# A hybrid decoder layer: state products, state update and masked products of each scan chunk issued in one run, and a reordered first layer norm

## The chip, the cores and the metric

The kernel runs on one core of a Trainium2 chip. The core has a matrix engine (TensorE, PE in the profile, with its weight loads as PEld), a vector engine (VectorE, DVE), a scalar engine (ScalarE, ACT), GpSimd (POOL) and SyncE (SP), which only issues DMAs here. Each engine works through its own instructions in order; between engines they wait by semaphores. The metric is the time of one execution on the device in microseconds, the median of several executions. Lower is better.

## What is computed

One layer: a layer norm at the input, a wide input projection, a conformer branch (a 31-tap causal convolution along time), a Mamba-2 state space branch in chunks of 128 positions, their gated mix with an output projection and a layer norm, and a gated feed-forward part with a short convolution. There are 1024 positions of 1024 channels, 32 heads of 64 channels, 4 groups with a state of 128.

```python
def ssd_chunked(x, dt, a_head, bm, cm):
    ...
    cb = jnp.einsum("bclgn,bcsgn->bcgls", cc, bc)
    y_diag = jnp.einsum("bcgrls,bcsgrp->bclgrp", cb[:, :, :, None] * decay, xs)
    decay_states = jnp.exp(a_cs[..., -1:] - a_cs)
    states = jnp.einsum("bclgn,bcgrl,bclgrp->bcgrpn", bc, decay_states, xs)
    chunk_decay = jnp.exp(a_cs[..., -1])
    ...
    y_off = jnp.einsum("bclgn,bcgrpn,bcgrl->bclgrp", cc, prev, jnp.exp(a_cs))
    return (y_diag + y_off).reshape(b, t, h, p)

def ssd_branch(z, xbc, dt_raw, conv_w, conv_b, dt_bias, a_log, d_skip, norm_w, w_out):
    ...
    xbc = jax.nn.silu(causal_dwconv(xbc, conv_w, conv_b))
    ...
    y = y + xh * d_skip.astype(jnp.float32)[:, None]
    yg = (y.reshape(bsz, t, SSM_DIM) * jax.nn.silu(z.astype(jnp.float32)))
    yg = yg.reshape(bsz, t, SSM_GROUPS, SSM_DIM // SSM_GROUPS)
    yg = yg * lax.rsqrt(jnp.mean(jnp.square(yg), axis=-1, keepdims=True) + RMS_EPS)
    yn = (yg.reshape(bsz, t, SSM_DIM) * norm_w.astype(jnp.float32)).astype(z.dtype)
    return yn @ w_out

def reference(x, ...):
    h = layer_norm(x, ln_in_g, ln_in_b)
    for l in range(DEPTH):
        u = h @ w_in[l]
        u_glu, z, xbc, dt_raw, gate_a, gate_b = split_in(u)
        y_a = conformer_branch(u_glu, ...)
        y_b = ssd_branch(z, xbc, dt_raw, ...)
        mix = (jax.nn.sigmoid(gate_a) * y_a + jax.nn.sigmoid(gate_b) * y_b) @ w_o[l]
        h = layer_norm(DN_ALPHA * h + mix, ln1_g[l], ln1_b[l])
        ffn = conv_ffn(h, w_ffn_up[l], ffn_dw_w[l], ffn_dw_b[l], w_ffn_down[l])
        h = layer_norm(DN_ALPHA * h + ffn, ln2_g[l], ln2_b[l])
    return h
```

## The kernel before

All matrices are f32. A large product is made of three fp32r matmuls of high and low parts (`mm3`, L180 to L182): high by high, high by low, low by high. `project` makes 24 of them, of 512 columns each, for 128 output channels. The high part is a cast on ACT (L146 for weights, L196 for activations), the low part a subtraction on DVE (L147, L197). The 1024 positions are taken in two halves (hh = 0 and 1) of 512.

`ln_first` norms the first half in four tiles of 128 positions, transposes each on TensorE (`hi`, `lo`) and makes the first three columns of the input projection (dt, and B and C of group 0) as soon as tiles are there (`columns`, q = 0 for the first two tiles, q = 1 for the others). On ACT, DVE and TensorE its order is that of the code (`manual_schedule`). Two tiles take their statistics on DVE (`stats`), two on ACT (`sums`).

`mixers` then goes over the four groups. For each group: the columns of B, C and four x tiles, each convolved by `conv4` (ACT and DVE) and passed through SiLU; the pending norm of the group before (`done`, which is `normed`); two columns of the conformer's gated unit; the scan of the group (`ssd_group`); the group's z gate (`z_gate`); and two pieces of the 31-tap convolution (`conv31`, L536 on DVE, 30 rows per piece), which have a low priority and fill DVE. For group 3 the first half of the scan's output projection (`ssm_out_first`, weights so_0 to so_7) stands ahead of it. `combine` makes the gate columns gb and the second half of that projection (sp_0 to sp_7), then the conformer's norm (mean at L763, variance) and its output.

A chunk of `ssd_group` is: four transposes of x (L584), a transpose of B (L587), CB (L590); on ACT the decay mask `m` (L598, L602) and the weighted x `xsd` (L613); on DVE the causal CB (`cbm`, L604), `xs` (L606) and the masked product `m` times `cbm` (L614); on TensorE four products with the carried state (`po`, L619), the state update (`pn`, L623) and eight masked products (`py`, L633), and on DVE the sums behind them (L620, L627, L630, L643). After four chunks come the skip (L648), the gate product with the SiLU of z (L652), squares and their sum (L654 to L658). `normed` sums them by channels on TensorE (L663), takes the root (L668, L669), sends the result through DRAM (`r_scr`, L671 and L672) so that it lies in all partitions, scales the tiles (L675) and splits them into `yT`.

The order of the instructions outside `manual_schedule` is set by the tile scheduler from priorities and an estimated timeline; the small products of a chunk are therefore strewn among the projections, which do not depend on them. Buffers bound how far the engines may part: four PSUM banks "acc" for projections, four "sm" for small products, three weight tiles, five `zs`, twelve `xbc`, two `m`, one `ys`.

Of the kernel before, what the change touches and what calls it, by code (L numbers as in the profile page):

```python
# [8 lines left out]
F32 = mybir.dt.float32  # L9
F32R = mybir.dt.float32r  # L10
AF = mybir.ActivationFunctionType
ALU = mybir.AluOpType
# [4 lines left out]
P = 128  # L17
D = 1024
# [26 lines left out]
RW_ING, RW_INB, RW_1G, RW_1B, RW_2G, RW_2B = (i * D for i in range(6))  # L45
# [4 lines left out]
CT_A, CT_G, CT_X, CT_B, CT_C, CT_DT, CT_GA, CT_GB = 0, 8, 16, 32, 36, 40, 41, 49  # L50
# [4 lines left out]
def kernel(  # L55
# [15 lines left out]
    V, A, G, TE, SY = nc.vector, nc.scalar, nc.gpsimd, nc.tensor, nc.sync  # L71
# [80 lines left out]
    def raw_weights(ct, name):  # L152
        st = wst.tile([P, D], F32, tag="st", name=f"st_{name}")
        SY.dma_start(st, wcol[ct])
        return st

    def split_weights(st, name):
        w = wsp.tile([P, 2, D], F32R, tag="w", name=f"w_{name}")
        A.copy(w[:, 0, :], st)
        V.tensor_tensor(  # L160
            out=w[:, 1, :], in0=st, in1=w[:, 0, :].bitcast(F32), op=ALU.subtract
        )
        return w
# [54 lines left out]
    def row(pl, start, n, name, tag=None):  # L218
        r = pl.tile([P, n], F32, tag=tag or name, name=name)
        SY.dma_start(r, prow[start : start + n].partition_broadcast(P))  # L220
        return r
# [21 lines left out]
    def ln_apply(t, mv, rs, i, g, b, op=ALU.subtract):  # L243
        V.scalar_tensor_tensor(  # L244
            out=t, in0=t, scalar=mv[:, i, 0:1], in1=g, op0=op, op1=ALU.mult
        )
        V.scalar_tensor_tensor(  # L247
            out=t, in0=t, scalar=rs[:, i : i + 1], in1=b, op0=ALU.mult, op1=ALU.add
        )

    def ln_first():
# [3 lines left out]
        with pool("lnin0", side="right") as pl:  # L255
            xts, raw = [], []
            with tc.high_priority(offset=8000), tc.manual_schedule(
                engines={et.Activation, et.DVE, et.PE}
            ):
                gb = [pl.tile([P, D], F32, name=n) for n in ("in_g", "in_b")]  # L260
                for r, start in zip(gb, (RW_ING, RW_INB)):
                    A.dma_start(r, prow[start : start + D].partition_broadcast(P))
                A.activation(out=pl.tile([P, 1], F32, name="warm"), in_=eps, func=AF.Sqrt)
                for t in range(4):
                    xt = pl.tile([P, D], F32, tag="x", bufs=4, name=f"x0_{t}")
                    SY.dma_start(xt, x[t * P : (t + 1) * P, :])
                    xts.append(xt)
                    if t:
                        raw.append(raw_weights((CT_DT, CT_B, CT_C)[t - 1], f"first{t}"))
                SY.dma_start(pc[:, :PC_N], pcol[:, :PC_N])  # L270
                SY.dma_start(a_log, prow[RW_AL : RW_AL + HEADS].partition_broadcast(P))
                SY.dma_start(nskip.rearrange("p i k -> p (i k)"), pcol[:, PC_N:])
# [12 lines left out]
                def sums(t):  # L285
                    mean, var = mvs[t][:, 0, 0:1], mvs[t][:, 0, 1:2]
                    A.activation(out=work, in_=xts[t], func=AF.Identity, accum_out=var)
                    A.mul(mean, var, -1.0 / D)
                    A.activation(out=work, in_=xts[t], func=AF.Square, bias=mean, accum_out=var)
                    A.activation(out=rss[t], in_=var, func=AF.Sqrt, bias=eps, scale=1.0 / D)  # L290

                def norm(t):
                    V.reciprocal(out=rss[t], in_=rss[t])
                    op = ALU.subtract if t < 2 else ALU.add
                    ln_apply(xts[t], mvs[t], rss[t], 0, *gb, op=op)
                    SY.dma_start(h_scr[0][t * P : (t + 1) * P, :], xts[t])

                def hi(t):
# [31 lines left out]

                stats(0)
                stats(1)
                norm(0)
                hi(0)
                norm(1)
                lo(0)
                ws.append(weights_side_by_side(raw[0], "c0_dt"))
                hi(1)
                lo(1)
                columns(0, 0, ((0, 0), (0, 1)))  # L340
                ws.append(split_weights(raw[1], "c0_b"))
                sums(2)
                columns(1, 0, ((0, 0), (0, 1), (1, 0)))
                norm(2)
                ws.append(split_weights(raw[2], "c0_c"))
                sums(3)
                norm(3)
                hi(2)
                columns(2, 0, ((0, 0), (0, 1), (1, 0)))
# [210 lines left out]
    def ssd_group(pl, hh, g, xT, BT, CT, gate):  # L560
# [16 lines left out]
        for c in range(4):  # L577
# [31 lines left out]
            if not last:  # L609
                xsd = pl.tile([P, HALF], F32, tag="xsd", name=f"xsd{nm}")  # L610
                for h in range(8):
                    hs, k = slice(h * HP, (h + 1) * HP), 8 * g + h
                    A.mul(xsd[:, hs], px[:, hs], dts[1][:, c, k : k + 1])  # L613
            V.tensor_tensor(out=m, in0=m, in1=cbm.unsqueeze(1).to_broadcast([P, 8, P]), op=ALU.mult)  # L614
            if not first:
                po = bank(0)
                for i in range(4):
                    ts = slice(i * P, (i + 1) * P)
                    TE.matmul(po[:, ts], S[:, ts], CT[:, cs], start=True, stop=True)  # L619
                V.tensor_tensor(out=acc[:, :, cs], in0=by_tile(po), in1=acc[:, :, cs], op=ALU.mult)  # L620
            if not last:
                pn = bank(0)
# [9 lines left out]
            for h in range(8):  # L632
                TE.matmul(  # L633
                    py[h % 2 * HP : (h % 2 + 1) * HP, h // 2 * P : (h // 2 + 1) * P],
                    xs[:, h * HP : (h + 1) * HP],
                    m[:, h, :],
                    start=True,
                    stop=True,
                )
            if first:  # L640
                A.copy(acc[:, :, cs], by_tile(py))
            else:
                V.tensor_tensor(out=acc[:, :, cs], in0=acc[:, :, cs], in1=by_tile(py), op=ALU.add)  # L643
# [764 lines left out]
```

## Time and profile before

| | us |
|---|---|
| median of 3 runs | 1956.8 (1955.83 to 1957.99) |
| the profiled execution, own time | 1956.2 |
| its span, first to last instruction | 1954.5 |
| TensorE busy | 1925.0 |
| VectorE busy | 1635.8 |
| ScalarE busy | 1106.4 |
| GpSimd busy | 133.1 |

A row of a timeline has the start, the duration, the engine, the line, the operation, the tiles written and read, the number of equal instructions taken together, and in brackets how long the engine was idle before and what released it. Durations of matmuls overlap, since they are pipelined; the distance of two starts is what one costs. A view of waits has a line for each pair of waiting and released line: the time in total, how often, and the longest.

### The profile page before, as it was taken

The numbers are of one execution on the slowest core, as the hardware profiler recorded it, in microseconds if no ns is written. First come the engines' busy times: TensorE is split into PE (matmuls) and PEld (weight loads), VectorE is DVE, ScalarE is ACT, GpSimd is POOL, SyncE is SP. The second block draws the span as 40 slices with busy tenths as digits, with TensorE's granted clock in tenths as the row PEclk, the third lists the DMA queues.
The fourth block names the chain that finished last, engine by engine and source line by source line (L and its number), as shares of the span: only waits on it lengthen the run. The fifth ranks groups of instructions, "written<-read, shape, count | busy, mean of one in ns | idle before, by whom it ended". The sixth has DMA issues, their size and how long they took to land.

```text
span 1954.5 us, 24929 instructions
## 1 busy us (share of the span) xinstructions
PE 1925.0 (98%) x9128; PEld 1574.9 (81%) x9128; DVE 1635.8 (84%) x2215; ACT 1106.4 (57%) x1841; POOL 133.1 (7%) x184
## 2 busy tenths in 40 slices
PE   6999999999999999999999999999999999999998
PEld 5888888887788887888888888888888888888886
DVE  7699999998666879999999966588998887887778
ACT  5767777565453268867755545365655454453442
POOL 0100000000400010000000040001000000021000
PEclk9999999999999999999999999999999999999999
DMA  6434343534445643434353454477443232377572
GB/s 215 129 114 130 107 137 101 186 115 140 162 135 192 230 122 107 145 109 135 98 177 109 136 180 130 154 265 256 151 162 108 103 113 87 108 242 260 183 252 108
DMA packets 104011, 297.68 MB, mean 152 GB/s; under 512 B 12432, under 2 KB 12464, under 8 KB 103888
## 3 DMA queue, kind: packets, MB, share of 16 engines
q1 hardware_dynamic: 87552, 243.63, 37.2%
q0 software_dynamic: 13744, 47.21, 7.8%
q10 hardware_dynamic: 2592, 5.24, 0.7%
q8 instruction: 71, 1.16, 0.2%
q14 instruction: 52, 0.43, 0.1%
HBM read 246.22 MB, written 49.82 MB: 151 GB/s over the span
## 4 chain that ended last, share of the span: by engine, by line
PE 80%; issue 11%; DVE 4%; ACT 2%; DMA 2%; POOL 1%; SPq 0%; ACTq 0%; DVEq 0%; POOLq 0%
PE acc L181 21%; PE acc L180 21%; PE acc L182 21%; PE sm L180 4%; PE sm L181 4%; PE sm L182 4%; PE sm L633 2%; PE sm L619 1%; PE sm L623 1%; PE sm L584 1%; DMA m<-cum_scr 1%; PE acc L323 1%; DVE rows L244 1%; POOL var L772 0%; DVE rows L247 0%
## 5 line engine op out<-in xcount | busy, mean ns | idle before, releaser
L536 DVE SCALAR_TENSOR_TENSOR c<-v,pc,c 128x512 f32<-128x512 f32 x480 | 344.3, 743 | 6.5 <-ACT c L525 5.3
L180 PE MATMUL acc<-hT,w_c 128*128 128x512 f32 x368 | 147.2, 400 | 0.0
L181 PE MATMUL acc<-hT,w_c 128*128 128x512 f32 x368 | 146.9, 399 | 0.0
L182 PE MATMUL acc<-hT,w_c 128*128 128x512 f32 x368 | 145.0, 394 | 0.0
L598 ACT ACTIVATE m<-m,cums 128x128 f32<-128x128 f32 x256 | 79.0, 396 | 66.1 <-DMA m<-cum_scr 61.8
L1043 DVE SCALAR_TENSOR_TENSOR fo<-u,pc,fo 128x1024 f32<-128x1024 f32 x88 | 111.1, 1285 | 0.0
L491 DVE SCALAR_TENSOR_TENSOR xbc<-u,pc,xbc 128x512 f32<-128x512 f32 x144 | 104.9, 744 | 1.1 <-ACT xbc L489 0.9
L180 PE MATMUL acc<-h1s,w_s 128*128 128x512 f32 x264 | 103.1, 391 | 0.0
L182 PE MATMUL acc<-h1s,w_s 128*128 128x512 f32 x264 | 103.0, 390 | 0.0
L182 PE MATMUL acc<-hT,w_z 128*128 128x512 f32 x256 | 102.8, 402 | 0.0
L181 PE MATMUL acc<-h1s,w_s 128*128 128x512 f32 x264 | 102.7, 389 | 0.0
L180 PE MATMUL acc<-hT,w_z 128*128 128x512 f32 x256 | 101.9, 398 | 0.4 <-ACT sig L512 0.4
L181 PE MATMUL acc<-hT,w_z 128*128 128x512 f32 x256 | 101.2, 395 | 0.0
L1183 ACT CAST w_dn<-dr 128x1024 fp32r<-128x1024 f32 (+1 forms) x73 | 60.8, 842 | 69.5 <-DVE dr L1113 38.5
L181 PEld LDWEIGHTS acc<-hT,w_c 128*128 128x128 f32 x368 | 69.2, 188 | 16.4 <-issue 3.1
L182 PEld LDWEIGHTS acc<-hT,w_c 128*128 128x128 f32 x368 | 69.1, 188 | 15.6 <-issue 1.9
L180 PEld LDWEIGHTS acc<-hT,w_c 128*128 128x128 f32 x368 | 69.2, 188 | 15.5 <-issue 1.9
L1184 DVE TENSOR_TENSOR w_dn<-dr,w_dn 128x1024 fp32r<-128x1024 f32 (+1 forms) x73 | 70.0, 968 | 11.6 <-ACT w_dn L1183 11.4
L147 DVE TENSOR_TENSOR w_c<-st_c,w_c 128x1024 fp32r<-128x1024 f32 x46 | 55.9, 1216 | 19.9 <-ACT w_c L146 19.9
L146 ACT CAST w_c<-st_c 128x1024 fp32r<-128x1024 f32 x46 | 48.3, 1051 | 40.3 <-PE acc L182 17.2
L180 PE MATMUL sm<-h1b,w_s 128*128 128x512 f32 x176 | 69.1, 393 | 0.0
L181 PE MATMUL sm<-h1b,w_s 128*128 128x512 f32 x176 | 69.0, 392 | 0.0
(380 smaller groups left out, 5592.0 us busy)
## 6 DMA issues: line engine op xcount, KB each, us to landing
st_c<-wcol SPq DMA_DIRECT2D x46, 512.0 KB, 3.5
st_z<-wz SPq DMA_DIRECT2D x32, 512.0 KB, 3.6
m<-cum_scr POOLq DMA_DIRECT2D x32, 512.0 KB, 4.9
st_wo<-wo SPq DMA_DIRECT2D x24, 512.0 KB, 4.3
ra<-wup SPq DMA_DIRECT2D x22, 512.0 KB, 3.5
rb<-wup SPq DMA_DIRECT2D x22, 512.0 KB, 3.3
t_scr<-fo POOLq DMA_DIRECT2D x22, 512.0 KB, 3.4
dr<-t_scr SPq DMA_DIRECT2D x44, 256.0 KB, 3.7
```

Source lines behind the costliest of these rows:

```text
L146: A.copy(w[:, 0, :], st)
L147: (eng or V).tensor_tensor(out=w[:, 1, :], in0=st, in1=w[:, 0, :].bitcast(F32), op=ALU.subtract)
L180: TE.matmul(ps, wa(0), xa(0), start=start, stop=False, skip_group_check=more)
L181: TE.matmul(ps, wa(0), xa(1), start=False, stop=False, skip_group_check=more)
L182: TE.matmul(ps, wa(1), xa(0), start=False, stop=stop, skip_group_check=more)
L491: V.scalar_tensor_tensor(out=o, in0=u[:, k : k + HALF], scalar=pc[:, wc + k : wc + k + 1], in1=o, op0=ALU.mult, op1=ALU.add,)
L536: V.scalar_tensor_tensor(out=accs[i], in0=v[:, k : k + HALF], scalar=pc[:, wc + k : wc + k + 1], in1=accs[i], op0=ALU.mult, op1=ALU.add,)
L598: A.activation(out=m[:, h, :], in_=m[:, h, :], func=AF.Relu, scale=-1.0, bias=cums[:, c, k : k + 1],)
L633: TE.matmul(py[h % 2 * HP : (h % 2 + 1) * HP, h // 2 * P : (h // 2 + 1) * P], xs[:, h * HP : (h + 1) * HP], m[:, h, :], start=True, stop=True,
L1043: V.scalar_tensor_tensor(out=o, in0=u[:, k : k + T], scalar=pc[:, wc + k : wc + k + 1], in1=o, op0=ALU.mult, op1=ALU.add,)
L1183: A.copy(w[:, 0, cs], src)
L1184: V.tensor_tensor(out=w[:, 1, cs], in0=src, in1=w[:, 0, cs].bitcast(F32), op=ALU.subtract)
```

## The change

Two places are edited. In `ln_first` the rows of the input norm's scale and shift (in_g, in_b) are loaded on SyncE's queue behind the first two x tiles instead of on ScalarE's queue, and the first raw weights move behind the third and fourth x tiles. The first two tiles are normed together (both subtractions, then both scalings), and the two `sums` move ahead in ScalarE's order: `sums(2)` ahead of the first cast, `sums(3)` ahead of the split of the C weights.

In `ssd_group` TensorE's part from the state products through the state update to the masked products is put under a `manual_schedule`, so that these run in the order of the code with nothing between them, and the first state product gets a dependency on the masked product of DVE, which only the masked products had before. The lines below L290 move: L584 is L593 after, L590 is L599, L614 is L623, L619 is L632, L623 is L645, L633 is L655, L648 is L671, L652 is L675, L663 is L686, L675 is L698.

```diff
--- before.py
+++ after.py
@@ -257,16 +257,15 @@
             with tc.high_priority(offset=8000), tc.manual_schedule(
                 engines={et.Activation, et.DVE, et.PE}
             ):
-                gb = [pl.tile([P, D], F32, name=n) for n in ("in_g", "in_b")]
-                for r, start in zip(gb, (RW_ING, RW_INB)):
-                    A.dma_start(r, prow[start : start + D].partition_broadcast(P))
                 A.activation(out=pl.tile([P, 1], F32, name="warm"), in_=eps, func=AF.Sqrt)
                 for t in range(4):
                     xt = pl.tile([P, D], F32, tag="x", bufs=4, name=f"x0_{t}")
                     SY.dma_start(xt, x[t * P : (t + 1) * P, :])
                     xts.append(xt)
-                    if t:
-                        raw.append(raw_weights((CT_DT, CT_B, CT_C)[t - 1], f"first{t}"))
+                    if t == 1:
+                        gb = [row(pl, RW_ING, D, "in_g"), row(pl, RW_INB, D, "in_b")]
+                    for ct in ((), (), (CT_DT, CT_B), (CT_C,))[t]:
+                        raw.append(raw_weights(ct, f"first{ct}"))
                 SY.dma_start(pc[:, :PC_N], pcol[:, :PC_N])
                 SY.dma_start(a_log, prow[RW_AL : RW_AL + HEADS].partition_broadcast(P))
                 SY.dma_start(nskip.rearrange("p i k -> p (i k)"), pcol[:, PC_N:])
@@ -289,10 +288,21 @@
                     A.activation(out=work, in_=xts[t], func=AF.Square, bias=mean, accum_out=var)
                     A.activation(out=rss[t], in_=var, func=AF.Sqrt, bias=eps, scale=1.0 / D)
 
-                def norm(t):
-                    V.reciprocal(out=rss[t], in_=rss[t])
-                    op = ALU.subtract if t < 2 else ALU.add
-                    ln_apply(xts[t], mvs[t], rss[t], 0, *gb, op=op)
+                def norm(*ts):
+                    for t in ts:
+                        V.reciprocal(out=rss[t], in_=rss[t])
+                        V.scalar_tensor_tensor(
+                            out=xts[t], in0=xts[t], scalar=mvs[t][:, 0, 0:1], in1=gb[0],
+                            op0=ALU.subtract if t < 2 else ALU.add, op1=ALU.mult,
+                        )
+                    for t in ts:
+                        V.scalar_tensor_tensor(
+                            out=xts[t], in0=xts[t], scalar=rss[t], in1=gb[1],
+                            op0=ALU.mult, op1=ALU.add,
+                        )
+                        store(t)
+
+                def store(t):
                     SY.dma_start(h_scr[0][t * P : (t + 1) * P, :], xts[t])
 
                 def hi(t):
@@ -330,20 +340,19 @@
 
                 stats(0)
                 stats(1)
-                norm(0)
+                norm(0, 1)
+                sums(2)
                 hi(0)
-                norm(1)
                 lo(0)
                 ws.append(weights_side_by_side(raw[0], "c0_dt"))
                 hi(1)
                 lo(1)
                 columns(0, 0, ((0, 0), (0, 1)))
                 ws.append(split_weights(raw[1], "c0_b"))
-                sums(2)
                 columns(1, 0, ((0, 0), (0, 1), (1, 0)))
                 norm(2)
+                sums(3)
                 ws.append(split_weights(raw[2], "c0_c"))
-                sums(3)
                 norm(3)
                 hi(2)
                 columns(2, 0, ((0, 0), (0, 1), (1, 0)))
@@ -611,12 +620,25 @@
                 for h in range(8):
                     hs, k = slice(h * HP, (h + 1) * HP), 8 * g + h
                     A.mul(xsd[:, hs], px[:, hs], dts[1][:, c, k : k + 1])
-            V.tensor_tensor(out=m, in0=m, in1=cbm.unsqueeze(1).to_broadcast([P, 8, P]), op=ALU.mult)
+            masked = V.tensor_tensor(
+                out=m, in0=m, in1=cbm.unsqueeze(1).to_broadcast([P, 8, P]), op=ALU.mult
+            )
+            run = ExitStack()
+            run.enter_context(tc.manual_schedule(engines={mybir.EngineType.PE}))
             if not first:
                 po = bank(0)
                 for i in range(4):
                     ts = slice(i * P, (i + 1) * P)
-                    TE.matmul(po[:, ts], S[:, ts], CT[:, cs], start=True, stop=True)
+                    mm = TE.matmul(po[:, ts], S[:, ts], CT[:, cs], start=True, stop=True)
+                    if i == 0:
+                        tc.add_manual_dep(
+                            mm.ins,
+                            masked.ins.name,
+                            mybir.DependencyInfo(
+                                mybir.DependencyClass.Sync, mybir.DependencyReason.DATA
+                            ),
+                            reason="state products run beside the masked ones",
+                        )
                 V.tensor_tensor(out=acc[:, :, cs], in0=by_tile(po), in1=acc[:, :, cs], op=ALU.mult)
             if not last:
                 pn = bank(0)
@@ -637,6 +659,7 @@
                     start=True,
                     stop=True,
                 )
+            run.close()
             if first:
                 A.copy(acc[:, :, cs], by_tile(py))
             else:
```

Three places of the program show what moves.

First, TensorE in group 1 of the first half, `project` rows L180 to L182 among the rows of a chunk. Before, the masked products of the third chunk (tiles m_1_2, xs_1_2) run into the transposes of the fourth, and the state products (state) stand one projection further:

```order
L180 MATMUL acc_2251<-hT_194,w_c_26_2254 128x512
L633 MATMUL sm_1813<-m_1_2_1778,xs_1_2_1791 64x128 [waits DVE_49,PE_49]
L633 MATMUL sm_1813<-m_1_2_1778,xs_1_2_1791 64x128 x7
L584 MATMUL sm_1823<-ident,xbc_4_1378 128x128
L584 MATMUL sm_1823<-ident,xbc_5_1418 128x128
L584 MATMUL sm_1823<-ident,xbc_6_1458 128x128
L584 MATMUL sm_1823<-ident,xbc_7_1498 128x128
L587 MATMUL sm_1828<-ident,xbc_17_1298 128x128
L181 MATMUL acc_2251<-hT_194,w_c_26_2254 128x512
L619 MATMUL sm_1858<-xbc_21_1338,state_120 128x128 [waits DVE_49]
```

After, at the end of the fourth chunk, L632 are the state products, L645 the update, L655 the masked products:

```order
L180 MATMUL acc_2950<-hT_194,w_c_35_2953 128x512
L632 MATMUL sm_1881<-xbc_21_1350,state_120 128x128 [waits DVE_49,PE_49]
L632 MATMUL sm_1881<-xbc_21_1350,state_120 128x128 x3
L645 MATMUL sm_1887<-xsd_1_3_1869,bt_1_3_1851 128x512
L655 MATMUL sm_1891<-m_1_3_1854,xs_1_3_1867 64x128 [waits PE_49]
L655 MATMUL sm_1891<-m_1_3_1854,xs_1_3_1867 64x128 x7
L181 MATMUL acc_2950<-hT_194,w_c_35_2953 128x512
```

The three kinds stand together; the transposes, the transpose of B and CB of a chunk stand ahead of it among the projections. The masked product's wait for DVE has passed to the first state product.

Second, what stands 20 projections behind that run on TensorE: the end of group 3's column of B (w_c_35), and the first matmul of its column of C (w_c_39), which waits for ScalarE:

```order
L180 MATMUL acc_2950<-hT_194,w_c_35_2953 128x512
L181 MATMUL acc_2950<-hT_194,w_c_35_2953 128x512
L182 MATMUL acc_2950<-hT_194,w_c_35_2953 128x512
L180 MATMUL acc_2990<-hT_194,w_c_39_2993 128x512 [waits Activation_49]
L181 MATMUL acc_2990<-hT_194,w_c_39_2993 128x512
```

Before, the same place has no wait; the last masked products of group 1 stand at row 938 of TensorE's order and this column at row 1128:

```order
L181 MATMUL acc_2914<-hT_194,w_c_35_2917 128x512
L182 MATMUL acc_2914<-hT_194,w_c_35_2917 128x512
L180 MATMUL acc_2954<-hT_194,w_c_39_2957 128x512
L181 MATMUL acc_2954<-hT_194,w_c_39_2957 128x512
L182 MATMUL acc_2954<-hT_194,w_c_39_2957 128x512 [waits DVE_49]
```

What TensorE waits for there is the last of these ScalarE rows (ss is the square of group 1's first gated tile, zs_2_1 a z gate of group 2, whose PSUM bank acc_2738 is the one to be reused; zs has five buffers):

```order
L497 COPY u_23_3020<-u_halo 128x3
L611 ACTIVATE m_2_1_2573<-m_2_1_2573 128x1024 [waits Activation_49]
L509 COPY u_halo<-u_19_2980 128x3 [waits Activation_49]
L677 ACTIVATE ss_1_2030<-xbc_4_1390 128x512 [waits DMASW0_49,DVE_49]
L565 ACT_TABLE_LOAD
L565 ACTIVATE zs_2_1_2799<-acc_2738 128x512
```

The z gate stands behind the square of group 1, which stands behind the scan's sums, skip and gate product on DVE. Before, the run from which they follow is far ahead of the column.

Third, TensorE around the norm of group 3 in the first half (ss_3, pick), w_gb_0 to w_gb_2 gate columns and w_sp_0 the second half of the scan's output projection, whose last twelve matmuls read group 3's yT. Before, the norm stands in the column gb_0, and that half begins 53 projections on:

```order
L182 MATMUL acc_4292<-hT_194,w_gb_0_4295 128x512
L180 MATMUL acc_4292<-hT_194,w_gb_0_4295 128x512
L663 MATMUL sm_4068<-ss_3_3917,pick 4x128 [waits DVE_49,PE_49]
L663 MATMUL sm_4068<-ss_3_3917,pick 4x128 x3
L181 MATMUL acc_4292<-hT_194,w_gb_0_4295 128x512
```

After, it stands in the column gb_2, eleven projections ahead of that half:

```order
L182 MATMUL acc_4439<-hT_194,w_gb_2_4442 128x512
L180 MATMUL acc_4439<-hT_194,w_gb_2_4442 128x512
L686 MATMUL sm_4116<-ss_3_3965,pick 4x128 [waits DVE_49]
L686 MATMUL sm_4116<-ss_3_3965,pick 4x128 x3
L181 MATMUL acc_4439<-hT_194,w_gb_2_4442 128x512
```

and then

```order
L181 MATMUL acc_4439<-hT_194,w_gb_2_4442 128x512
L182 MATMUL acc_4439<-hT_194,w_gb_2_4442 128x512
L180 MATMUL acc_4406<-yT_2_3454,w_sp_0_4409 128x512 [waits Activation_49]
L181 MATMUL acc_4406<-yT_2_3454,w_sp_0_4409 128x512 [waits DVE_49]
L182 MATMUL acc_4406<-yT_2_3454,w_sp_0_4409 128x512
```

The first matmul of w_sp_0 here reads the high part of group 3's first tile and waits for ScalarE, the next the low part and waits for VectorE.

## The prediction

> **What bounds the kernel now.** I read the page first, then the waits of TensorE, then timelines of the places that the change touches.
>
> ```profile
> span 1954.5 us, 24929 instructions
> PE 1925.0 (98%) x9128; PEld 1574.9 (81%) x9128; DVE 1635.8 (84%) x2215; ACT 1106.4 (57%) x1841; POOL 133.1 (7%) x184
> PEclk9999999999999999999999999999999999999999
> ```
>
> TensorE is busy for 98% of the span at the full granted clock. Time can be won only by giving it less to do or by starting it sooner, and every wait that it gets is paid in full. The view of waits says how little it waits now:
>
> ```profile
> PE sm L204 <- DVE x L247: 16.0, 3, 13.3
> PE acc L180 <- ACT first L965: 1.0, 1, 1.0
> PE sm L619 <- DVE state L630: 0.9, 1, 0.9
> PE sm L763 <- POOL mean L761: 0.6, 1, 0.6
> ```
>
> The columns are total, number and longest. 16.0 us lie in the head, before the first transposes; in the whole of the scan TensorE waited once, for 0.9 us. So the question is what becomes late when its order changes. The scale for that is the pitch of the projection matmuls that fill the stream:
>
> ```profile
> 491.00 0.39 PE L182 MATMUL acc<-hT,w_gb 128*128 128x512 f32 x1
> ...
> 495.08 0.39 PE L182 MATMUL acc<-hT,w_gb 128*128 128x512 f32 x1
> ```
>
> From the first to the second are 18 pitches (three matmuls for each step of k), 4.08 us, so 0.2267 us each. DVE at 84% is no bound as a whole, yet its queue is long: each chain below stands among conv31 rows.
>
> **The change part by part. Fewer interruptions of the projections.** In the order of before a chunk's small products stand in three places, in the changed one mostly in two (state products, state update, masked products in one piece). In the whole stream the pieces between projections fall from 134 to 116, 18 fewer. What a lone piece costs is seen at a state update:
>
> ```profile
> 330.35 0.39 PE L182 MATMUL acc<-hT,w_c 128*128 128x512 f32 x1
> 330.58 1.02 PE L623 MATMUL sm<-xsd,bt 128*128 128x512 f32 x2
> 331.04 0.79 PE L180 MATMUL acc<-hT,w_c 128*128 128x512 f32 x1
> 331.67 0.40 PE L181 MATMUL acc<-hT,w_c 128*128 128x512 f32 x1
> ```
>
> From 330.35 to 331.67 are 1.32 us where two pitches would be 0.45, so the update takes 0.87 us. Two passes that start 0.46 us apart account for nearly all of it; the edge of a piece can be at most the 0.40 by which the last pitch (0.63) exceeds 0.23. Gain: 18 pieces by 0 to 0.40 us, 0 to 7.2; I take 0.09 each, **−1.6**, near the lower end because the two starts explain the rest.
>
> **The added wait for the mask.** The first state product now waits for the masked product on DVE; behind it on TensorE stand all later projections, and behind those the casts and convolutions that read them. Two chunks of before, in which the mask is early and late:
>
> ```profile
> 750.64 0.38 PE L590 MATMUL sm<-xbc,xbc 128*128 128x128 f32 x2
> ...
> 758.67 1.22 DVE L614 TENSOR_TENSOR m<-m,cbm 128x1024 f32<-128x1024 f32 x1
> ...
> 1093.52 0.39 PE L590 MATMUL sm<-xbc,xbc 128*128 128x128 f32 x2
> 1100.09 1.22 DVE L614 TENSOR_TENSOR m<-m,cbm 128x1024 f32<-128x1024 f32 x1
> 1103.63 1.09 PE L633 MATMUL sm<-m,xs 128*64 128x128 f32 x16
> ```
>
> From CB's start to the mask's end passed 9.25 and 7.79 us. In the changed order 27 to 61 projections (6.1 to 13.8 us) stand between CB and the first state product in all chunks but one, so I cost the wait at nothing there; DVE's mask is hidden by those projections. Where the cover is gone it costs the difference. That is the first chunk of group 2 in the second half: 16 projections lie between (3.6 us), and on DVE the mask stands behind the four rows that scale the outputs of group 1, which wait for their norm by DMA. By the chain quoted below, these four start 8.5 us and the mask ends some 13.5 us after the norm matmul, while TensorE is there after about 10.3 (37 projections and CB, bt and transposes): 2.1 to 5.4 us, taken **3.2**. In the first half the same boundary delays a bank of ssm_out by 0 to 1.7, taken **0.6**.
>
> **Group 3's C column behind group 2's gate.** Here the move itself makes a wait. Since the chunks are spread over more projections, group 1's last run now ends 20 projections ahead of the column of C (25 in the second half), instead of some 180. That column takes the bank of a z gate whose SiLU needs a buffer that is freed by the gate product of group 1. What lies between shows at the end of a group in before:
>
> ```profile
> 465.51 1.09 PE L633 MATMUL sm<-m,xs 128*64 128x128 f32 x16
> 466.65 0.69 DVE L643 TENSOR_TENSOR ys<-ys,sm 128x512 f32<-128x512 f32 x1 [0.93 <-PE sm L633]
> 467.92 2.73 DVE L648 SCALAR_TENSOR_TENSOR xbc<-xbc,nskip,ys 128x512 f32<-128x512 f32 x4
> 472.37 2.49 DVE L652 TENSOR_TENSOR xbc<-xbc,zs 128x512 f32<-128x512 f32 x4
> 473.98 0.62 ACT L654 ACTIVATE ss<-xbc 128x512 f32<-128x512 f32 x1
> 274.06 1.28 ACT L556 ACT_TABLE_LOAD   x1
> 275.35 0.60 ACT L556 ACTIVATE zs<-acc 128x512 f32<-128x512 f32 x1
> ```
>
> Counted from the start of the run: state products and update take 1.8 us, the masked run 1.1; sum added 1.1 behind its start and 0.7 long (3.6 now); skip, 2.7 with conv31 rows ahead (8 to 9); the first gate product after two more conv31 rows (10.5 to 11); the square that stands ahead on ACT 0.6; table 1.28; SiLU 0.6: ready 13.4 to 15.6 us after the run's start. TensorE is there after 2.9 + 20 × 0.2267 = 7.4. So 6.0 to 8.2, taken **6.8**; second half, where the run has no state update: there after 2.1 + 25 × 0.2267 = 7.8, ready after 13.3 to 14.5, so 5.5 to 6.7, taken **6.3**.
>
> **The second half of sp_0 behind group 3's norm.** The norm matmul of group 3 moves from 53 to 11 projections ahead of the first row that reads its result (17 in the second half). The chain in before:
>
> ```profile
> 485.57 1.04 PE L663 MATMUL sm<-ss,pick 128*4 128x128 f32 x8
> 486.64 0.36 ACT L668 ACTIVATE rr<-sm,eps 4x128 f32<-4x128 f32 x1 [0.39 <-PE sm L663]
> 487.04 0.94 DVE L669 RECIPROCAL rr<-rr 4x128 f32<-4x128 f32 x1 [1.31 <-ACT rr L668]
> 494.08 2.74 DVE L675 SCALAR_TENSOR_TENSOR xbc<-xbc,nskip,ss 128x512 f32<-128x512 f32 x4 [1.71 <-DMA ss<-r_scr]
> 494.87 1.95 ACT L196 CAST yT<-xbc 128x512 fp32r<-128x512 f32 x3 [3.75 <-DVE xbc L675]
> ...
> 496.74 1.89 DVE L197 TENSOR_TENSOR yT<-xbc,yT 128x512 fp32r<-128x512 f32 x3
> ```
>
> The first scaled tile is cast at 494.87 + 0.6, 9.9 us after the norm; the first low part follows at 497.4 (11.9) and the fourth at about 13.7, most of it the two DMAs over r_scr between 488 and 494. In before TensorE had 53 × 0.2267 = 12.0 us of other rows. Now the last of the twelve products of that half could end after 1.2 + 23 × 0.2267 = 6.4 us and will end at about 14.2. Nothing else can run: three gate projections and sp_0 hold the four banks. Stall 6.4 to 8.5, taken **7.8**; second half, with 17 projections ahead and a chain of 8.9 to the scaled tile, 5.3 to 8, taken **6.8**. The two mean matmuls (L763, 0.6 us in before) get 0 to 2.8 each, taken 1.0, **2.0** in all, since their loads pass a changed SP queue.
>
> **The clock after such stalls.** In the head the first eight transposes ran after 13.3 us of idleness, later ones after 2.2:
>
> ```profile
> 13.33 1.94 PE L204 MATMUL sm<-ident,x 128*128 128x128 f32 x8 [13.33 <-DVE x L247]
> 15.82 1.79 PE L204 MATMUL sm<-ident,x 128*128 128x128 f32 x8 [0.54 <-DVE x L247]
> 24.92 1.07 PE L204 MATMUL sm<-ident,x 128*128 128x128 f32 x8 [2.17 <-DVE x L247]
> ```
>
> The slow pieces cost 0.87 + 0.72 = 1.6 us more, although the page's clock row shows no dip. Four stalls (two at the C column, two at sp_0) are 6 to 8 us, between the two cases: 0 to 1.6 each. They are almost midway between 2.2 and 13.3, so I take half, 0.8 by four, **3.2**.
>
> [...]
>
> **The head.** The loads of in_g and in_b go from ACT's queue to SP's behind x0 and x1; x2, x3 and the first weights come behind them.
>
> ```profile
> 9.12 1.29 DVE L224 BATCH_NORM_STATS2 st_in<-x 128x6 f32<-128x512 f32 x2 [1.42 <-DMA x<-x]
> 10.60 1.27 DVE L244 SCALAR_TENSOR_TENSOR x<-x,mv_in,in_g 128x1024 f32<-128x1024 f32 x1
> 26.00 1.27 DVE L244 SCALAR_TENSOR_TENSOR x<-x,mv_in,in_g 128x1024 f32<-128x1024 f32 x1
> 30.04 2.08 PE L323 MATMUL acc<-hT,w_c_dt 128*64 128x256 f32 x16 [0.24 <-ACT hT L301]
> in_b<-prow ACTq DMA_DIRECT2D x1, 512.0 KB, 8.2
> ```
>
> x1 arrived at 9.1 and set the first norm; in_b, issued at 1.25, landed at about 9.5 beside it. Without 1 MB ahead of it x1 comes some 2.5 us sooner, but the norms then wait for in_b behind it, at an unchanged 9.5: the first transposes come at about 12 instead of 13.33. What counts is the last of the four tiles, whose norm (26.00) waited for its sums on ACT. These sums pass a cast of 1.05 us and the earlier tile's sums pass the first casts, so that norm starts at about 23.4, and the columns of 30.04 at 27.5: −0.5 to −4, taken **−2.4**.
>
> **Sum**, against the profiled execution's own 1956.2 us (span 1954.5 and 1.7 around it; the median of the runs, 1956.8, is the same within 0.03%): C column 13.1, norm boundary 3.8, sp_0 14.6, means 2.0, clock 3.2, pieces −1.6, head −2.4: +32.7, **1989 us**. With all terms at their lower ends (11.5 + 2.1 + 11.7 + 0 + 0 − 7.2 − 4 = 14) 1970, at their upper ends (14.9 + 7.1 + 16.5 + 5.6 + 6.4 + 0 − 0.5 = 50) 2006.
>
> **The rivals.** *Nothing becomes late (faster).* The stalls at the C column and sp_0 are computed with chains of before, taken while DVE ran conv31 rows in between. If the scheduler's spreading leaves DVE and ACT empty at these points, the waits vanish and only pieces and head remain: 1956.2 − 4.0 = 1952. It decides at 7.4 us from the run to the SiLU and at about 3.5 us from norm to cast. Against it: the bare durations of the first chain (1.8 + 1.1 + 0.7 + 2.7 + 0.6 + 0.6 + 1.3 + 0.6) are 9.4 already, and the second holds two DMAs. Chance 0.08.
>
> *Half of it.* The two chains run at their bare length: 2.0 us at each C column, and at sp_0, if the r_scr trip falls by 3 us, 4 each: 12 + 3.8 − 4 → 1968. Chance 0.14, of which a third ends near no change if the head gives its full 4.
>
> *The mask is late everywhere.* If DVE, pressed by the rows that arrive together behind each run, ends the mask 1 us behind TensorE in each of 31 chunks, that is 31 us more: 2020. It decides where the 7.8 to 9.3 us above exceed the 6.1 to 13.8 between CB and the run. For it speaks the shortest distance, against it that in before TensorE never waited for the mask: the masked products start 2.3 us behind its end in the quoted chunk (1101.31 to 1103.63), and the view of waits has no row for it. Chance 0.12.
>
> [...] Chance 0.28; the forecast itself 0.38.
>
> **How the numbers follow.** The forecast and its neighbour with the slow clock hold 0.66 between 1970 and 2006. To hold 8 in 10 the range reaches down into the half case and up to the beginning of the late masks: 1966 to 2009. What a measurement of this kernel can tell from no change is about 0.2%, 3.9 us. Faster by more: the first rival and a little of the second, 0.09; the same: 0.05; slower: 0.86.
>
> **What would show it.** In the waits of TensorE after: a projection waiting for the SiLU of z, twice, 5 to 8 us; sp_0 waiting for yT, twice, in pieces that sum to 5 to 8.5; the state products waiting for the mask once for 2 to 5 and hardly elsewhere; the columns after the head at 27 to 29 us. Pitches of 0.45 instead of 0.23 behind those waits would show the slow clock. I am wrong if the state products wait for the mask in many chunks, or if sp_0 finds yT ready.

## The result, and the profile after

| | before | changed |
|---|---|---|
| median, us | 1956.9 (1955.83 to 1957.99) | 1987.33 (1985.98 to 1992.67) |
| span of the profiled execution, us | 1954.5 | 1985.1 |
| TensorE busy, us | 1925.0 | 1934.4 |
| mean granted clock of TensorE | 0.999 | 0.992 |

The changed kernel takes 1.0161 times as long, 95% interval 1.0148 to 1.0174, so it is 1.6% slower. The forecast was 1989 (1966 to 2009). The sign and the size came out, but two of the steps behind it did not hold as written, and a third had the wrong size.

The view of TensorE's waits in the changed kernel (total, number, longest):

```profile
PE sm L204 <- DVE x L299: 11.8, 1, 11.8
PE acc L180 <- ACT yT L196: 11.1, 2, 6.4
PE acc L180 <- ACT xbc L498: 8.9, 3, 4.7
PE sm L632 <- DVE m L623: 2.7, 2, 2.2
PE acc L181 <- DVE yT L197: 2.3, 2, 1.1
...
PE sm L655 <- DVE m L623: 0.9, 1, 0.9
```

The wait in the head has become 4.2 us shorter. New are 13.4 us for group 3's yT in sp_0, 8.9 us for rows of the convolution (xbc, L498), and 3.6 us for the mask. Of the 8.9 us, 4.67 and 3.07 lie at the C column of group 3, once in each half, and 1.15 ahead of the first half's ssm_out (331.45). L498 is not the row that the prediction and the front part named for the C column. TensorE's timeline there, with what stands on POOL's queue and ScalarE:

```profile
286.19 0.54 POOL L602 DMA_DIRECT2D m<-cum_scr  x1 [23.40 <-DVE c L545]
290.02 0.39 PE L182 MATMUL acc<-hT,w_c 128*128 128x512 f32 x1
290.56 2.46 ACT L607 ACTIVATE m<-m,cums 128x128 f32<-128x128 f32 x8 [7.16 <-DMA m<-cum_scr]
...
294.34 0.68 ACT L498 ACTIVATE xbc<-acc,pc 128x512 f32<-128x512 f32 x1
295.07 0.80 PE L180 MATMUL acc<-hT,w_c 128*128 128x512 f32 x1 [4.67 <-ACT xbc L498]
295.67 0.63 PE L181 MATMUL acc<-hT,w_c 128*128 128x512 f32 x1
...
299.27 0.60 ACT L565 ACTIVATE zs<-acc 128x512 f32<-128x512 f32 x1
```

The last run of group 1 ends at 285.65 and frees a mask buffer. Only then is the next mask loaded (286.19; the row's bracket names a row of VectorE, but e9 below shows that it is the buffer that holds the load up); ScalarE stands still for 7.16 us at its first step, and behind that step stand the copies of the B column, which release a PSUM bank at 295.02. TensorE goes on at 295.07. The SiLU that the prediction had in mind comes only at 299.27: it was late, as forecast, but TensorE got another bank sooner.

The pitch after the wait is 0.43 instead of 0.23 us. The windows of TensorE (start and end, length, busy, granted clock, DMA share and GB/s) give the clock:

```profile
285.00:290.00 5.00, 5.00 (x31) 1.00 0.50 161
...
295.00:298.00 3.00, 2.93 (x7) 0.50 0.32 87
298.00:301.00 3.00, 3.00 (x15) 0.98 1.04 217
508.00:515.00 7.00, 0.56 (x4) 0.87 0.46 157
515.00:519.80 4.80, 3.65 (x8) 0.50 0.26 68
519.80:523.00 3.20, 3.20 (x15) 0.97 0.88 292
```

After each of the four waits, of 4.67 and 3.07 us at the C column and of 6.44 and 4.62 us in sp_0, 0.50 or 0.51 of the clock is granted for 3 to 6 us; the longest is behind the C column of the second half, where the pitch is 0.43 us from 954.69 until 960.2 (granted clock 0.50):

```profile
954.10 0.79 PE L180 MATMUL acc<-hT,w_c 128*128 128x512 f32 x1 [3.07 <-ACT xbc L498]
```

The last three windows are around sp_0, whose chain went as written:

```profile
504.71 1.04 PE L686 MATMUL sm<-ss,pick 128*4 128x128 f32 x8
513.47 2.74 DVE L698 SCALAR_TENSOR_TENSOR xbc<-xbc,nskip,ss 128x512 f32<-128x512 f32 x4 [2.64 <-DMA ss<-r_scr]
514.25 2.61 ACT L196 CAST yT<-xbc 128x512 fp32r<-128x512 f32 x4 [4.69 <-DVE xbc L698]
514.92 0.80 PE L180 MATMUL acc<-yT,w_sp 128*128 128x512 f32 x1 [6.44 <-ACT yT L196]
516.87 0.80 PE L181 MATMUL acc<-yT,w_sp 128*128 128x512 f32 x1 [1.15 <-DVE yT L197]
```

From the norm matmul to the first cast's end are 10.2 us (9.9 were read from before), 6.1 of them the trip over DRAM (from POOL's issue at 507.41 to the scaling at 513.47).

### The profile page after: what moved, and what is told of

It is laid out like the page before. It is cut to its first block, busy times and chain, and to the rows that moved or that the text cites. A ratio compares the mean times of both kernels' runs of the same rounds, so it can differ in the third digit from the quotient of the medians.

```text
span 1985.1 us, 24892 instructions
## 1 busy us (share of the span) xinstructions
PE 1934.4 (97%) x9128; PEld 1580.5 (80%) x9128; DVE 1641.4 (83%) x2215; ACT 1090.2 (55%) x1828; POOL 133.7 (7%) x184
## 4 chain that ended last, share of the span: by engine, by line
PE 69%; issue 14%; DVE 8%; ACT 4%; DMA 3%; POOL 1%; SPq 0%; DVEq 0%; POOLq 0%; ACTq 0%
PE acc L181 18%; PE acc L180 18%; PE acc L182 18%; PE sm L180 3%; PE sm L182 3%; PE sm L181 3%; DVE c L545 2%; PE sm L655 1%; DMA m<-cum_scr 1%; PE sm L632 1%; PE sm L645 1%; ACT m L607 1%; PE acc L333 1%; PE sm L593 1%; DMA ss<-r_scr 1%
## 5 line engine op out<-in xcount | busy, mean ns | idle before, releaser
L180 PE MATMUL acc<-hT,w_c 128*128 128x512 f32 x368 | 146.9, 399 | 7.7 <-ACT xbc L498 7.7
L182 PE MATMUL acc<-hT,w_c 128*128 128x512 f32 x368 | 145.2, 395 | 0.0
L180 PE MATMUL acc<-h1s,w_s 128*128 128x512 f32 x264 | 103.1, 391 | 0.0
L182 PE MATMUL acc<-h1s,w_s 128*128 128x512 f32 x264 | 103.0, 390 | 0.0
L182 PE MATMUL acc<-hT,w_z 128*128 128x512 f32 x256 | 101.1, 395 | 0.0
L180 PE MATMUL acc<-hT,w_z 128*128 128x512 f32 x256 | 100.5, 392 | 0.0
L180 PEld LDWEIGHTS acc<-hT,w_c 128*128 128x128 f32 x368 | 70.2, 191 | 23.5 <-ACT xbc L498 8.6
L182 PEld LDWEIGHTS acc<-hT,w_c 128*128 128x128 f32 x368 | 70.1, 191 | 14.4
L180 PE MATMUL sm<-h1b,w_s 128*128 128x512 f32 x176 | 69.1, 393 | 0.0
L181 PE MATMUL sm<-h1b,w_s 128*128 128x512 f32 x176 | 69.0, 392 | 0.0
L182 PE MATMUL sm<-h1b,w_s 128*128 128x512 f32 x176 | 69.0, 392 | 0.0
```

Source lines behind the costliest of these rows:

```text
L180: TE.matmul(ps, wa(0), xa(0), start=start, stop=False, skip_group_check=more)
L181: TE.matmul(ps, wa(0), xa(1), start=False, stop=False, skip_group_check=more)
L182: TE.matmul(ps, wa(1), xa(0), start=False, stop=stop, skip_group_check=more)
```

## The experiments

Medians, with the kernel before at 1956.3 to 1956.7 us in the same sessions; ratios are to it.

| kernel | us | ratio, 95% interval |
|---|---|---|
| e1, head alone | 1953.32 | 0.9982 (0.9973 to 0.9992) |
| e2, scan part alone | 2001.34 | 1.0229 (1.0214 to 1.0245) |
| e3, schedule without the wait | 1952.12 | 0.9979 (0.9969 to 0.9989) |
| e8, wait without the schedule | 1986.87 | 1.0152 (1.0135 to 1.0169) |
| e6, not in group 3 | 1973.28 | 1.0085 (1.0070 to 1.0100) |
| e7, in group 3 alone | 1959.02 | 1.0017 (1.0007 to 1.0026) |
| e4, six z gate buffers | 1994.07 | 1.0192 (1.0177 to 1.0207) |
| e5, three mask buffers | 1988.23 | 1.0162 (1.0147 to 1.0177) |
| e9, mask load of its own | 1982.27 | 1.0127 (1.0111 to 1.0144) |
| e10, head alone, TensorE kept busy | 1954.94 | 0.9994 (0.9985 to 1.0004) |

**Head and scan apart.** In e1 `ssd_group` is that of before, in e2 `ln_first` is.

> The head of the change alone; the scan is that of before. Theory 1 (the loss lies in a few stalls in the scan and the head is a pure gain): the columns of the last two tiles come 4.2 us sooner, as in the changed kernel (25.85 against 30.04), nothing later waits for them, and the time is 1956.9 - 4.2 = 1952.7 us. Rival (the earlier start is eaten up later, since weights and gates come no sooner): within 1 us of 1956.9.

> The scan's part of the change alone, with the head of before. Theory 1: 1987.3 + 4.2 = 1991.5 us, 1988 to 1995, since some chunks of group 2 come out in other places; TensorE stalls again at the C column of group 3 (some 5 and 3 us) and in sp_0 (8 and 6.5 us), each followed by pitches of 0.43 us. Rival (head and scan part are tied together, the shifted start is what makes the engines collide): well under 1988, with the stalls at the C column gone.

The head is a gain: 1953.32, 3.0 us under before (4.6 in the session of e3, which has the same order). The scan's part alone costs 45 us, 10 more than theory 1 had (its waits at the C column and in sp_0 are there, as stated). The surplus is a third place, in group 2 of the first half, in the timeline of e2 (POOL's queue, ScalarE, TensorE):

```profile
334.93 0.54 POOL L593 DMA_DIRECT2D m<-cum_scr  x1 [7.73 <-ACT w_so L146]
338.78 2.45 ACT L598 ACTIVATE m<-m,cums 128x128 f32<-128x128 f32 x8 [1.60 <-DMA m<-cum_scr]
345.11 1.83 ACT L489 ACTIVATE xbc<-acc,pc 128x512 f32<-128x512 f32 x3
345.83 0.79 PE L180 MATMUL acc<-yT,w_so 128*128 128x512 f32 x1 [9.15 <-ACT xbc L489]
```

It is the same chain (mask load, mask step, rows of the convolution behind it, a bank), 9.15 us long. In this order the second chunk of group 2 follows the first within 22 projections instead of 61. The head thus moves the scan's order too; the two parts do not simply add.

**Which edit of the scan moves it.** e3 takes out the dependency, e8 the manual schedule:

```diff
 # e3
-                    mm = TE.matmul(po[:, ts], S[:, ts], CT[:, cs], start=True, stop=True)
-                    if i == 0:
-                        tc.add_manual_dep(
...
+                    TE.matmul(po[:, ts], S[:, ts], CT[:, cs], start=True, stop=True)
 # e8
-            run.enter_context(tc.manual_schedule(engines={mybir.EngineType.PE}))
```

> The changed kernel with the manual schedule of the three kinds of products, but without the added wait of the first state product. Its instructions stand in the order of the head alone on every engine. Theory W (the added wait alone moves the chunks, and the loss follows from it): the time of the head alone, 1953.3 us within 2, and no wait for yT or at the C column. Rival (running the products under the manual schedule costs by itself): between 1953 and 1987.

> The changed kernel with the added wait of the first state product, but without the manual schedule. Its instructions stand in the order of the changed kernel on every engine. Theory W: the time of the changed kernel, 1987.3 us within 3, with the same waits (C column 4.8 and 3.2, yT 8.3 and 6.5 us). Rival: under 1980.

Both came out as theory W has it: 1952.12 and 1986.87. The view of TensorE's waits shows no yT and no L498 in e3, of which these are the first two lines:

```profile
PE sm L204 <- DVE x L299: 11.9, 1, 11.9
PE sm L632 <- DVE state L643: 1.1, 1, 1.1
```

In e8 it has the lines of the changed kernel:

```profile
PE acc L180 <- ACT yT L196: 11.1, 2, 6.6
PE acc L180 <- ACT xbc L498: 8.8, 3, 4.6
PE sm L631 <- DVE m L623: 2.3, 1, 2.3
PE acc L181 <- DVE yT L197: 2.3, 2, 1.1
```

So the manual schedule changes nothing here. All of the scan's loss follows from one dependency, and that although the wait itself is on TensorE for 3.6 us only. By the code, it puts the chain of a chunk's mask in series with the chain of its state: the state product, the update behind it and so the next chunk all follow the mask now. That this is why the scheduler spreads the chunks is inferred, not shown.

**The sp_0 stall.** e6 and e7 restrict both edits to groups 0 to 2 and to group 3 (`if g < 3` and `if g == 3` ahead of the schedule and of the dependency).

> The changed kernel without the added wait and the manual schedule in group 3, with both in groups 0 to 2. The norm matmul of group 3 then stands 57 to 60 projections ahead of the rows that read its result. Theory 1 (the sp_0 stalls with their slow clock are 19.6 us of the loss): 1987.3 - 19.6 = 1968 us, no wait for yT. Rival (the loss is spread over all chunks, each of which pays for its wait): a quarter of 34 us less, about 1979.

> The changed kernel with the added wait and the manual schedule in group 3 alone. The norm of group 3 stands 35 projections (first half) and 51 (second half) ahead of the rows that read its result, between 11 or 17 in the changed kernel and 53 or 66 in before. Theory 1: the chain from the norm to the first cast is 10.2 us long, so the first half stalls for 1 to 3 us and the second not, without a slow clock: 1952.7 + 2 = 1954.7, 1953 to 1957; no stall at the C column. Rival (each chunk pays): 1952.7 + a quarter of 34, about 1961.

In e6 the wait for yT is gone and the time falls by 14 us to 1973.28, more than the 8.5 of the rival, less than the 19.6 of theory 1. Most of what is missing is a new wait for L498, of 3.96 us with slow pitches behind it (granted clock 0.57 from 986.6 to 990), in group 2 of the second half. The time alone does not decide between the two; the view of waits does, since TensorE waits for the mask for 0.5 us only. In e7 the first half waits a little, as expected, but slow pitches follow that were not; TensorE's timeline there:

```profile
501.82 0.61 PE L180 MATMUL acc<-yT,w_sp 128*128 128x512 f32 x1 [2.12 <-ACT yT L196]
503.76 0.79 PE L181 MATMUL acc<-yT,w_sp 128*128 128x512 f32 x1 [1.33 <-DVE yT L197]
504.35 0.63 PE L182 MATMUL acc<-yT,w_sp 128*128 128x512 f32 x1
```

The window of TensorE behind it has the clock (length, busy, granted clock, DMA share, GB/s):

```profile
504.00:509.00 5.00, 4.91 (x12) 0.51 0.54 186
```

Two waits of 2.1 and 1.3 us with one matmul between them sufficed for half the clock (0.51). With these pitches 1959.0 us came out instead of the expected 1954.7. That is nearer to the rival's 1961, but in e7's view of waits no row waits for the mask, so the chunks do not each pay. Over these runs the first wait for yT follows the distance: 11 projections between norm and use gave 6.4 us (changed kernel), 17 gave 4.6 (its second half), 35 gave 2.1 (e7), 57 or more none (e6).

**The C column.** e4 sets `bufs=6` for zs, e5 `bufs=3` for m (two places), and e9 gives the load a tile of its own:

```diff
 # e9
+            mr = pl.tile([P, 8, P], F32, tag="mr", name=f"mr{nm}")
             G.dma_start(
-                mf, cum_scr[hh][g, c].rearrange("h l -> (h l)").partition_broadcast(P)
+                mr.rearrange("p h l -> p (h l)"), cum_scr[hh][g, c].rearrange("h l -> (h l)").partition_broadcast(P)
             )
...
-                    out=m[:, h, :], in_=m[:, h, :], func=AF.Relu, scale=-1.0,
+                    out=m[:, h, :], in_=mr[:, h, :], func=AF.Relu, scale=-1.0,
```

> The changed kernel with six z gate buffers instead of five. Theory 1a (the prediction's: the C column of group 3 waits for the SiLU of a z gate, held up by a buffer that group 1's gate product frees): both waits at the C column, 4.8 and 3.2 us with their slow pitches, are gone. Theory 1b (by the trace: it waits for the copies of the B column on ScalarE, which stand behind the decay mask's first step, which waits for the mask's load, which waits for the masked products that free its buffer): both waits stay, 4 to 5 and 3 to 4 us, released by L498. The time is no guide here, since chunks of group 2 and the norms of group 3 fall in other places (nearer sum by theory 1b about 1988, by 1a about 1977).

> The changed kernel with three decay mask buffers instead of two. The last run of group 1 then stands 44 projections ahead of the C column in the first half, and 25 as before in the second; the mask step that stands ahead of the copies of B is one chunk further on, and its buffer is again the one freed by that run. Theory 1b: from the run's end to the copies' end pass 13 us (issue 0.6, load 4.4, step 2.5, casts 2, table and exponential 2.3, copies 1.2), so about 3 us of waiting in the first half and 5 to 7 in the second, and no gain in all: 1983 to 1992. Theory 1a: nothing changes in the second half, 3.2 us.

> The changed kernel with a buffer of its own for the mask's load, so that the load waits for no masked product; the first step writes from it into the mask's buffer. At the C column of the first half 22 projections stand behind group 1's run, as 20 in the changed kernel, and the same step stands ahead of the copies of B, now with the table and exponential also ahead. Theory 1b: without issue and load (5 us), with 2.3 more of table and exponential, the wait falls from 4.8 to about 2 us, and TensorE's waits for the copies of the convolution (8.9 us) by half. Theory 1a: the wait stays 4.8 or grows. The sp_0 halves stand 24 and 19 projections behind the norm, instead of 11 and 17: 3 us and 1 less there.

With six z gate buffers TensorE does not wait at the C column, in either half, although ScalarE is blocked by the load exactly as before. Timeline of e4:

```profile
277.77 0.60 ACT L565 ACTIVATE zs<-acc 128x512 f32<-128x512 f32 x1
290.35 0.39 PE L182 MATMUL acc<-hT,w_c 128*128 128x512 f32 x1
290.57 0.39 PE L180 MATMUL acc<-hT,w_c 128*128 128x512 f32 x1
291.04 2.47 ACT L607 ACTIVATE m<-m,cums 128x128 f32<-128x128 f32 x8 [7.33 <-DMA m<-cum_scr]
294.83 0.69 ACT L498 ACTIVATE xbc<-acc,pc 128x512 f32<-128x512 f32 x1
```

The second z gate is through at 278.4 instead of 299.9, its bank is free, and the column starts at 290.57, at once. Theory 1b, that the blocked copies alone make the wait, is refuted in that form. With the load out of the chain (e9) it is issued at 265.10 instead of 286.19, and the wait fell as 1b had said, from 4.67 to 2.21 us; ScalarE and TensorE in e9:

```profile
286.29 2.46 ACT L608 ACTIVATE m<-mr,cums 128x128 f32<-128x128 f32 x8 [2.38 <-PE sm L656]
...
292.69 0.69 ACT L498 ACTIVATE xbc<-acc,pc 128x512 f32<-128x512 f32 x1
...
293.43 0.50 PE L180 MATMUL acc<-hT,w_c 128*128 128x512 f32 x1 [2.21 <-ACT xbc L498]
```

In the second half the wait is gone. Theory 1a, by which it stays 4.8 us or grows, is refuted by this one. All waits for L498 fell less than the half that was expected, from 8.9 to 5.7 us, since 3.5 us are new ahead of ssm_out. What is left is both together: the z gates without a buffer hold three of the four banks, and the column takes the bank that is free sooner, by the SiLU of a z gate (e4, 278.4) or by the copies behind the mask's load (changed kernel, 295.02 against 299.87). e5 waits 3.1 us more than a pitch in both halves: the first as expected, the second was priced too high (5 to 7) and is what theory 1a had said, so e5 does not separate the two. None of the three gains much, since other waits take the place: e9 is 5 us under the changed kernel, and e4 comes to 1994.07 with waits of 6.3 and 5.1 us for the same L498 rows in group 2.

**The clock.** e10 adds, ahead of the first tile in e1's head, work for an idle TensorE that nothing reads:

```diff
+                idle = bank(0)
+                for i in range(64):
+                    TE.transpose(idle[:, i % 4 * P : (i % 4 + 1) * P], ident, ident)
```

> The head of the change alone, with 64 transposes of the identity into an unread bank on TensorE ahead of the first tile's, in its idle time (from 2 to about 10 us); the kernel's results do not use them. Theory C (an idle TensorE runs at half its clock for some 4 us afterwards): the 16 transposes of the first two tiles take 1.8 us instead of 3.4, and the kernel gains 0.5 to 1.6 us against the head alone (1953.3), as far as ScalarE and VectorE follow. Rival (these transposes are slow for another cause, such as their first use of the tiles or the traffic of the loads): 3.4 us as before, and no gain.

TensorE's timeline in the head of e10:

```profile
1.68 8.80 PE L343 MATMUL sm<-ident 128*128 128x128 f32 x64 [1.68 <-POOL ident masks.py:199]
11.91 2.29 PE L204 MATMUL sm<-ident,x 128*128 128x128 f32 x16 [1.43 <-DVE x L299]
...
25.95 2.07 PE L333 MATMUL acc<-hT,w_c_dt 128*64 128x256 f32 x16 [0.24 <-ACT hT L311]
```

The 16 transposes take 2.29 us (1.8 were expected) instead of 3.54 in e1's profile, behind 1.43 us of idleness instead of 11.80, so it is the idleness ahead of them that slows them. The granted clock does not show it: it is 1.00 in the windows of both heads. The expected gain in time did not come (1954.94 against 1953.32; the columns of the last tiles start at 25.95 against 26.02): in both kernels those columns wait for ScalarE's cast (hT, L311).

## Why the prediction came out, step by step

| term | predicted, us | measured, us |
|---|---|---|
| sp_0 behind group 3's norm | 14.6 | 13.4 (L196 11.1, L197 2.3) |
| C column of group 3 | 13.1 | 7.7 (4.67 and 3.07) |
| boundary of group 2 | 3.8 | 4.2 (L632 2.2, L655 0.9, bank of ssm_out 1.15) |
| mask elsewhere | 0 | 0.5 |
| mean matmuls | 2.0 | 0 |
| slow clock | 3.2 | about 8 |
| fewer pieces | −1.6 | about −0.4 |
| head | −2.4 | −4.2 |
| sum | 32.7 | 29 of 30.4 |

*The wait for the mask* behaved as forecast, at the place that was named and with 2.21 us of the 3.2 taken (2.1 to 5.4 were said; TensorE's timeline of the changed kernel):

```profile
988.64 1.13 PE L632 MATMUL sm<-xbc,state 128*128 128x128 f32 x8 [2.21 <-DVE m L623]
```

Elsewhere it is hidden by projections, but for 0.9 us at 327.66 and 0.5 at 760.75; the rival in which every chunk pays (2020) is out, by this view and by e7. But the prediction laid the spread of the chunks to the products in one piece. e3 and e8 show that the dependency does it alone. The front part of this document and its first table of rows should be read so too: the products stand together because the first of them waits, not because of the schedule.

*sp_0* held in mechanism and size; e6 takes it away, e7 and the other distances scale it.

*The C column* is the step that failed as written: "That column takes the bank of a z gate whose SiLU needs a buffer that is freed by the gate product of group 1." The first SiLU of group 2's waiting z gates was ready 17.2 us after the run's start at 282.71 (13.4 to 15.6 were said) and was not what released TensorE. A shorter chain, overlooked, came first: buffer of the mask, load, the step on ScalarE, and the copies of B behind it. So the wait was 4.7 and 3.1 us, not 6.8 and 6.3. The buffers of z do matter, as e4 shows, but only as one half of the cause.

*The clock* was mis-sized: the excess of the pitches behind the four stalls over 0.2267, summed from their starts, is about 1.5, 1.5, 3.0 and 1.9 us, instead of 0.8 each. Taking half of the 1.6 us was the error. The windows behind the four show a granted clock of 0.50 or 0.51. How long the slow stretch lasts does not follow from the wait: the one behind 954.10, after the shortest of the four (3.07 us), lasted the longest, 6 us, and in e9 a wait of 2.2 us was enough for one (last section).

*The pieces* gained next to nothing. A whole piece of state products, update, masked products and transposes costs 3.38 us by the starts of the projections around it, its parts one by one some 3.5.

*The head* gained more than forecast, and by the step that was named: the norm of the last tile started at 21.81 instead of 26.00 us (23.4 were said), and the columns of the last tiles moved from 30.04 to 25.85 in the changed kernel's timeline.

```profile
11.75 3.42 PE L204 MATMUL sm<-ident,x 128*128 128x128 f32 x16 [11.75 <-DVE x L299]
25.85 2.08 PE L333 MATMUL acc<-hT,w_c_dt 128*64 128x256 f32 x16 [0.24 <-ACT hT L311]
```

That the sum came within 2 us of the time is luck in part: the C column was 5 us too dear, the clock 5 to 7 us too cheap. Counted from start to start, with one pitch of 0.2267 us taken off for each matmul, the four stalls with their slow stretches cost 6.4, 9.9, 6.2 and 8.4 us, 30.9 in all; the table has 29.0 for them. So the clock is rather 10 us than 8, and with that the terms add up to 31, within 1 us of the measured 30.4. Why the scheduler spreads the chunks as far as it does (in e6 and e4 other chunks of group 2 move) was not followed further. Of the kernels run, the head alone (e1, and e3 with the same order) is the fastest, 0.2% under before.

## What to carry to other kernels

A dependency can cost many times its own wait: this one is 3.6 us of waiting in a loss of 34 (1987.3 against the 1953.3 of e1), and the rest came from what moved behind it, a norm that came too close to its reader and a buffer that came free too late. When a bound engine is fed by in-order engines, look for what stands behind a wait for DMA in their queues: a copy that frees a PSUM bank behind a step that waits for a load stalls TensorE just as the load would (4.67 us at 295.07). For two releases that could free the same resource, work out both chains; the sooner sets the wait (here 295.02 against 299.87).

## What the runs showed of the hardware

In e9 TensorE's clock dropped after a wait much shorter than the 6 to 8 us for which the prediction weighed it, and with a delay. The projections waited 2.2 us (2.6 between two starts, 290.83 and 293.43), ran at a pitch of 0.23 to 0.34 us for about 1 us, and then at about half the clock (0.53; windows of TensorE, columns as above):

```profile
290.80:293.40 2.60, 0.42 (x2) 1.00 0.38 142
293.40:295.00 1.60, 1.57 (x6) 0.81 0.14 23
295.00:298.00 3.00, 3.00 (x9) 0.53 1.00 238
298.00:301.00 3.00, 3.00 (x15) 1.00 1.02 261
```

In the head of before a wait of 2.17 us (24.92) had no such effect (eight transposes in 1.07 us, granted clock 1.00 from 24.9 to 30), nor had the one of 2.21 at 988.64 of the changed kernel (granted clock 1.00 from 986 to 992). The clearest pair is in e5, where the C column waits 2.94 us in the first half and 2.91 in the second (windows of TensorE right behind the two waits):

```profile
294.00:296.00 2.00, 1.86 (x8) 1.00 1.02 211
950.80:953.00 2.20, 2.10 (x6) 0.60 0.49 194
```

The first keeps the full clock, 1.00, the second falls to 0.60 in its window. So in these runs, between 2.2 and 2.9 us, the length of the wait alone does not tell whether it happens; what decides stays open. In e9 the slow stretch cost some 1.7 us, almost as much as the wait.
